# A state-space mixer inside a two-layer decoder: SiLU through Tanh, decay tiles prepared group by group, and a new order of the projections around z

## The chip, the cores and the metric

The kernel runs on one core of one Trainium2 chip. The metric is the device time of one execution in microseconds (us); lower is better. A core has five engines that run side by side, each through its own queue in order: TensorE (PE in the profile, with its weight loads shown apart as PEld), VectorE (DVE), ScalarE (ACT), GpSimd (POOL), and SyncE (SP), whose queue issues most transfers. An instruction waits at the head of its queue until what it needs is there, and everything behind it waits too.

## The reference

A trunk of two layers works on 256 tokens of 1024 features, all in 32-bit floats. Each layer is FFN, token mixer, cross-attention into 256 memory tokens, FFN. The mixer of layer 0 is differential attention. That of layer 1 is a Mamba-2 state-space mixer, and the change lies there alone:

```python
proj = h @ w_in                                   # 1024 -> 2048 z, 2048 xs, 1024 B, 1024 C, 32 dt
xbc = silu(causal_depthwise_conv(xbc, conv_w, conv_b))       # 4 taps along time
dt = softplus(dt + dt_bias); A = -exp(A_log)
a_cs = cumsum(dt * A) within chunks of 128 tokens
decay = exp(where(tril, a_cs[l] - a_cs[s], -inf))            # 32 heads x 2 chunks x 128 x 128
y_diag = (C B^T * decay) @ (xs * dt)                         # 8 groups of 4 heads share B and C
states = B^T (exp(a_cs[-1] - a_cs) * dt * xs);  y_off = exp(a_cs) * (C @ states of the chunk before)
y = (y_diag + y_off + D * xs) * silu(z)
y = y * rsqrt(mean over each group's 256 features of y^2 + eps) * gnorm;  return y @ w_out
```

## The kernel before

All products of weights run at full precision as three matmuls: a weight piece `w` is split into a rounded `whi` (ScalarE, L183) and the difference `wlo = w - whi` (VectorE, L184), and likewise the activations. Such a piece is 128x1024 elements and is called a gran here. Four `whi` and four `wlo` buffers and four weight buffers `w` rotate; a weight buffer is free for the next load when its pieces have been split, and SyncE's queue issues the loads in order. `proj` and `wide` (L199 on) append units, each a list of grans and a function with the matmuls; `proj` takes an `eng`, on which the difference of a unit's second gran is then made.

In the mixer (`ssd`), layer 1 runs 4 rounds. Round i serves groups 2i and 2i+1. It projects b and c for both groups (256 columns each), then xs (two units of 256 columns, one a group), then z for both. The small work on each group hangs on a planner, `pipe`: `pipe.after(us, f)` puts f into the program that many microseconds of planned matmul time later. The order of TensorE's instructions is exactly the order in which they are written, through these delays. The order on the other engines is set by the scheduler of the tile library at build time.

The steps of a group g, with the names that the profile shows:

- `conv`: ScalarE scales the newest tap out of PSUM (L1035), VectorE adds three older taps for each of two halves (L1042, 128x255, 254, 253), ScalarE applies SiLU with the bias (L1047). This is done for b, c (per round) and xs (per group).
- The decay tiles `E`, 128x512 for each group and chunk, come from a small DRAM buffer `scr` through SyncE's queue (L1006). ScalarE turns them with four `Relu` (L1020, 128x128 each) and one `Exp` (L1024).
- `cross` on TensorE: `tb` turns b, `pcb` is C B^T (L1096, L1101). VectorE masks it to `cbm` (L1107) and multiplies it into both E tiles (L1109).
- `turn_x`: TensorE turns xs into `tx` (L1116), ScalarE copies it to `xn` (L1120), GpSimd makes `xd = xn*dt`, `xe = xd*dte` and `xn*D` (L1124 to L1128).
- `inner`: `pst` (the state) and `py` (L1137, L1142). `state`: `pof` (L1156). `gate`: the sums and the product with `zs` = SiLU(z) (L1090, L1163 to L1165), the squares, `yrc` (a power on GpSimd, L315), the scaling, and `turn_y` with `ty` (L1185), whose result `y_hi`, `y_lo` feeds the output projection `out`.

SiLU, Exp and Tanh are evaluated from function tables in ScalarE; where the next function is not in the loaded set, the build puts an ACT_TABLE_LOAD before it.

Of the kernel before, what the change touches and what calls it, by code (L numbers as in the profile page):

```python
# [15 lines left out]
P = 128  # L16
# [41 lines left out]
def trunk(ctx, tc, a, out):  # L58
# [251 lines left out]
    def rpow(src, scale, n, name):  # L310

        m = sm.tile([P, 16], F32, name="msq", tag="msq")
        nc.vector.tensor_scalar(m[:, :n], src, scale, EPS, op0=ALU.mult, op1=ALU.add)  # L313
        c = sm.tile([P, 16], F32, name=name, tag=name)
        nc.gpsimd.tensor_tensor(c[:, :n], m[:, :n], neghalf[:, :n], op=ALU.pow)  # L315
        return c
# [593 lines left out]
    def ssd(norm, nxt, kv):  # L910
# [8 lines left out]
        dte = const.tile([P, 32], F32, name="dte")  # L919
        E = {}  # L920
# [29 lines left out]
        def dt_steps(pd):  # L950
            xd = const.tile(d32, F32, name="dtx")
            u = const.tile(d32, F32, name="dtu")
            s = const.tile(d32, F32, name="dts")
            s2 = const.tile(d32, F32, name="dts2")
            nega = const.tile([P, 32], F32, name="nega")
            for t in range(2):
                v.tensor_tensor(xd[:, t, :], pd[t], dtb, op=ALU.add)

            v.scalar_tensor_tensor(u, xd, -1.0, xd, op0=ALU.mult, op1=ALU.min)
            tc.keep_in_program_order(nc.scalar.activation(nega, alog, AF.Exp))  # L960

            def second():
                nc.scalar.activation(u, u, AF.Exp)
                pipe.after(1.0, third)

            def third():
                v.tensor_scalar(s, u, 2.0, None, op0=ALU.add)
                v.reciprocal(s, s)
                v.tensor_tensor(s, s, u, op=ALU.mult)
                v.tensor_tensor(s2, s, s, op=ALU.mult)  # L970
                v.tensor_scalar(dt, s2, 2.0 / 17, None, op0=ALU.mult)
                for c in (15, 13, 11, 9, 7, 5, 3):
                    v.scalar_tensor_tensor(dt, dt, 2.0 / c, s2, op0=ALU.add, op1=ALU.mult)
                v.scalar_tensor_tensor(dt, dt, 2.0, s, op0=ALU.add, op1=ALU.mult)
                v.scalar_tensor_tensor(dt, xd, 0.0, dt, op0=ALU.max, op1=ALU.add)
                v.scalar_tensor_tensor(av, dt, -1.0, nega.unsqueeze(1).broadcast_to(d32), op0=ALU.mult, op1=ALU.mult)
                pipe.after(5.0, sums)
            pipe.after(1.0, second)

        def sums():  # L980
# [9 lines left out]
            def out_of_psum():  # L990
# [35 lines left out]
        def conv(ps, ch, name, wait):  # L1026
# [18 lines left out]
            def silu():  # L1045
                for j in range(2):
                    nc.scalar.activation(o[:, j, :], o[:, j, :], AF.Silu, bias=cb_[:, ch[j]:ch[j] + 1])  # L1047
            pipe.after(evac, taps)
            pipe.after(wait, silu)
            return o  # L1050

# [22 lines left out]
        def group(g):  # L1074
# [3 lines left out]
            def xs_fin(ps):  # L1078
                s["xs"] = conv(ps, (2 * g, 2 * g + 1), "xs", 6.5)
                if g == 0:  # L1080
                    s["zs"] = held.pop()
                    pipe.after(6.5, lambda: nc.scalar.activation(s["zs"], s["zs"], AF.Silu))
                pipe.after(9.5, turn_x)

            def z_fin(ps):
                zs = v2(slot("zs"))

                def go():
                    for t in range(2):
                        nc.scalar.activation(zs[:, t, :], ps[t], AF.Silu)  # L1090
# [3 lines left out]
            def cross():  # L1094
# [8 lines left out]
                def go():  # L1103
                    s["bn"] = work("bn", P)
                    nc.scalar.copy(s["bn"], tb[:, 0:P])
                    cbm = work("cbm", S).rearrange("p (c l) -> p c l", c=2)
                    v.tensor_tensor(cbm, pcb[:, 0:2, :], triu.unsqueeze(1).broadcast_to([P, 2, P]), op=ALU.mult)  # L1107
# [4 lines left out]
            def turn_x():  # L1112
# [5 lines left out]
                def go():  # L1118
# [10 lines left out]
                                            dsk[:, hs].unsqueeze(1).unsqueeze(3).broadcast_to(bh), op=ALU.mult)  # L1129
                    s.update(xn=xn, xd=xd, xe=xe)  # L1130
                    pipe.after(8.5, inner)
                pipe.after(evac, go)

            def inner():
# [10 lines left out]
                def go():  # L1145
# [4 lines left out]
                    pipe.when(2.5, lambda: "zs" in s, state)  # L1150
                pipe.after(evac, go)

            def state():
# [7 lines left out]
                def gate():  # L1161
                    yo = work("yo", S)
                    v.tensor_tensor(r4(yo), r4(pof), b4(eacs[:, hs]), op=ALU.mult)  # L1163
# [13 lines left out]
                pipe.after(evac + 7.0, lambda: rc.append(rpow(ss[:, 0:2], 1.0 / 256, 2, "yrc")))  # L1177
# [188 lines left out]
```

## Time and profile before

| | |
|---|---|
| median of 3 runs | 1316.27 us (1316.23 to 1316.58) |
| the profiled execution | 1315.35 us, its span in the profile 1313.6 us |
| TensorE busy | 1296.7 us of the span (99%) |
| VectorE, ScalarE, GpSimd busy | 807.7, 738.5, 67.8 us (61%, 56%, 5%) |
| granted TensorE clock, mean | 0.996 |
| the mixer of layer 1 | about 798 us to 1035 us of the span |

A busy share near 1 on TensorE over the whole span says that a change elsewhere can matter only where TensorE stands still or runs at a lower clock. The queries used are: busy time by stretches of the span, the waits of TensorE, the groups of instructions by line, and the timeline of single engines. In a row of a group, the numbers behind the bar are total busy time and the mean of one instruction in ns, and behind the second bar the idle time of the engine just before them with what ended it.

### The profile page before, as it was taken

Reading aid. Unit: us, or ns where it says so; the run is one execution under the profiler, and the core shown is the slowest. Engines: PE = TensorE matmul, PEld = TensorE weight load, DVE = VectorE, ACT = ScalarE, POOL = GpSimd, SP = SyncE. Lnnn points to the kernel's source line nnn. Section 1 sums busy time; section 2 is a strip of 40 time slices with the busy share of each in tenths; the row PEclk is TensorE's granted clock in tenths of the full one; section 3 lists DMA queues with packets and bytes.
Section 4 is the critical chain, followed back from the end, with each engine's and each line's share of the span. In section 5 each row is a group of like instructions: output and inputs, shape, how many; then the busy total and the mean of one; then the engine's idle time right before and its main releaser. Section 6 shows DMA issues by size and latency. Waiting matters only on the chain.

```text
span 1313.6 us, 17832 instructions
## 1 busy us (share of the span) xinstructions
PE 1296.7 (99%) x6997; PEld 1115.4 (85%) x6997; DVE 807.7 (61%) x1178; ACT 738.5 (56%) x1208; POOL 67.8 (5%) x67
## 2 busy tenths in 40 slices
PE   9999999999999999999999999989999999999998
PEld 7888888788988888888888889889998898888887
DVE  5655456876665555555556456667885775655554
ACT  6456444685455444445445447999774664544432
POOL 1000002210000000000000000022311000000000
PEclk9999999999999999999999999999999999999999
DMA  9565565425445554656555546744534445655551
GB/s 325 187 219 182 178 198 173 154 102 191 161 142 176 186 173 130 234 182 217 172 186 189 187 152 216 225 156 129 186 136 160 161 161 161 197 173 175 208 177 49
DMA packets 134631, 232.02 MB, mean 177 GB/s; under 512 B 5737, under 2 KB 34066, under 8 KB 134546
## 3 DMA queue, kind: packets, MB, share of 16 engines
q1 hardware_dynamic: 133648, 229.75, 53.2%
q8 instruction: 55, 0.90, 0.3%
q10 hardware_dynamic: 738, 0.59, 0.1%
q0 software_dynamic: 160, 0.52, 0.1%
q14 instruction: 30, 0.25, 0.0%
HBM read 229.77 MB, written 1.08 MB: 176 GB/s over the span
## 4 chain that ended last, share of the span: by engine, by line
PE 88%; ACT 6%; DVE 3%; issue 1%; POOL 1%; DMA 1%; SPq 0%; POOLq 0%; ACTq 0%; DVEq 0%
PE out L221 7%; PE out L223 7%; PE out L222 7%; PE up L222 6%; PE up L223 6%; PE up L221 6%; PE gate L223 5%; PE gate L221 5%; PE gate L222 5%; ACT whi L183 2%; PE htp L611 1%; PE fin L221 1%; PE fin L223 1%; PE fin L222 1%; PE xq L222 1%
## 5 line engine op out<-in xcount | busy, mean ns | idle before, releaser
L184 DVE TENSOR_TENSOR wlo<-w,whi 128x1024 fp32r<-128x1024 f32 (+2 forms) x446 | 523.7, 1180 | 415.4 <-ACT whi L183 413.7
L183 ACT CAST whi<-w 128x1024 fp32r<-128x1024 f32 (+1 forms) x448 | 447.6, 1006 | 473.3 <-PE out L223 147.0
L222 PE MATMUL up<-wlo,xh 128*128 128x512 f32 x320 | 124.7, 390 | 0.1
L223 PE MATMUL up<-whi,xl 128*128 128x512 f32 x320 | 124.6, 389 | 0.0
L221 PE MATMUL up<-whi,xh 128*128 128x512 f32 x320 | 124.6, 389 | 0.0
L221 PE MATMUL gate<-whi,xh 128*128 128x512 f32 x312 | 123.3, 395 | 0.0
L222 PE MATMUL gate<-wlo,xh 128*128 128x512 f32 x312 | 121.7, 390 | 0.0
L223 PE MATMUL gate<-whi,xl 128*128 128x512 f32 x312 | 121.7, 390 | 0.0
L221 PE MATMUL out<-whi,hid_hi 128*128 128x512 f32 x264 | 103.6, 392 | 0.0
L223 PE MATMUL out<-whi,hid_lo 128*128 128x512 f32 x264 | 102.9, 390 | 0.0
L222 PE MATMUL out<-wlo,hid_hi 128*128 128x512 f32 x264 | 102.9, 390 | 0.0
L222 PEld LDWEIGHTS up<-wlo,xh 128*128 128x128 f32 x320 | 60.1, 188 | 13.0 <-DVE wlo L184 0.5
L221 PEld LDWEIGHTS up<-whi,xh 128*128 128x128 f32 x320 | 60.1, 188 | 12.5
L223 PEld LDWEIGHTS up<-whi,xl 128*128 128x128 f32 x320 | 60.1, 188 | 12.4
L223 PEld LDWEIGHTS gate<-whi,xl 128*128 128x128 f32 x312 | 58.6, 188 | 12.2
L222 PEld LDWEIGHTS gate<-wlo,xh 128*128 128x128 f32 x312 | 58.7, 188 | 11.9 <-POOL wlo L184 0.4
L221 PEld LDWEIGHTS gate<-whi,xh 128*128 128x128 f32 x312 | 58.7, 188 | 11.5
L223 PEld LDWEIGHTS out<-whi,hid_lo 128*128 128x128 f32 x264 | 49.6, 188 | 10.4
L222 PEld LDWEIGHTS out<-wlo,hid_hi 128*128 128x128 f32 x264 | 49.6, 188 | 10.0
L221 PEld LDWEIGHTS out<-whi,hid_hi 128*128 128x128 f32 x264 | 49.6, 188 | 10.0
L315 POOL TENSOR_TENSOR rcol<-msq,neghalf 128x2 f32<-128x2 f32 x8 | 5.6, 696 | 686.8 <-DVE msq L313 686.8
L221 PE MATMUL fin<-whi,hid_hi 128*128 128x512 f32 (+1 forms) x110 | 38.3, 348 | 0.0
(354 smaller groups left out, 2735.9 us busy)
## 6 DMA issues: line engine op xcount, KB each, us to landing
w<-in_ffn_w_up_dram SPq DMA_DIRECT2D x40, 1024.0 KB, 5.0
w<-in_ffn_w_down_dram SPq DMA_DIRECT2D x40, 1024.0 KB, 5.0
w<-in_ffn_w_gate_dram SPq DMA_DIRECT2D x38, 1024.0 KB, 5.0
w<-in_ssd_w_in_dram SPq DMA_DIRECT2D x24, 1024.0 KB, 5.3
w<-in_xa_w_kv_dram SPq DMA_DIRECT2D x16, 1024.0 KB, 5.0
w<-in_da_w_in_dram SPq DMA_DIRECT2D x12, 1024.0 KB, 5.1
w<-in_xa_w_q_dram SPq DMA_DIRECT2D x8, 1024.0 KB, 5.1
w<-in_xa_w_o_dram SPq DMA_DIRECT2D x8, 1024.0 KB, 4.9
```

The lines of the kernel that those rows point to most:

```text
L183: nc.scalar.copy(hv, src)
L184: self.eng.tensor_tensor(self.lo[:, :, o:o + n], src, hv.bitcast(F32), op=ALU.subtract)
L221: nc.tensor.matmul(o, lhsT=lh, rhs=rh, start=start, stop=False)
L222: nc.tensor.matmul(o, lhsT=lh, rhs=rl, start=False, stop=False)
L223: nc.tensor.matmul(o, lhsT=ll, rhs=rh, start=False, stop=stop)
L315: nc.gpsimd.tensor_tensor(c[:, :n], m[:, :n], neghalf[:, :n], op=ALU.pow)
L611: nc.tensor.transpose(tp[:, j, t * P:(t + 1) * P], us[t][:, (i + j) * P:(i + j + 1) * P], ident)
```

## The change

1. SiLU(x) is computed as x/2 times (1 + tanh(x/2)). The factor one half is left out of the products and put elsewhere: dt, D and the copies of b and of C B^T carry it (`dt*0.5`, `dskh`, `bn*0.5`, `0.25` at cbm, `0.5` at yo, and the normalization's eps times 4). One ScalarE Tanh of 128x512 and one VectorE product of 128x512 (`th`, L1064 and L1065 of the changed kernel) stand for two SiLU of 128x256. For z there are two Tanh and two products of 128x256 (L1059, L1061). The conv's bias moves into the first tap.
2. The decay tiles of group g are loaded 16 planned us before a time `at` of their own and turned just before it; before, groups 0 to 3 went first, all together.
3. The second group's xs stands behind z in rounds 0 to 2, and xs weights come in two loads of 256 columns.
4. The difference of the second gran of each b and c unit is made on GpSimd (8 grans).
5. The delays: b's SiLU after 6.5 in place of 12.3, `cross` after 12.0 and 18.0 more (6.0 in the last round) in place of 10.0 and 2.5, `turn_x` after 11.5 in place of 9.5, `state` after 3.2 in place of 2.5.

```diff
-                    pipe.after(0.5 if g < 4 else 24.0 + 7.0 * (g - 4), lambda g=g: spread(g))
+                    at = (9.0, 36.0, 47.0, 64.5, 80.5, 98.0, 114.0, 120.0)[g]
+                    pipe.after(max(0.5, at - 16.0), lambda g=g: spread(g))
                     for c in range(2):
-                        i = 2 * g + c
-                        pipe.after(6.0 + 1.3 * i if g < 4 else 33.0 + 4.0 * (i - 8), lambda g=g, c=c: decay(g, c))
-                    pipe.after((14.0, 16.0, 33.5, 36.0, 67.5, 70.0, 72.5, 75.0)[g], lambda g=g: decay2(g))
+                        pipe.after(max(6.0, at - 4.5) + 1.5 * c, lambda g=g, c=c: decay(g, c))
+                    pipe.after(at, lambda g=g: decay2(g))
...
-                    nc.scalar.activation(o[:, j, :], ps[:, j, :], AF.Copy, scale=tap(3, j))
+                    nc.scalar.activation(o[:, j, :], ps[:, j, :], AF.Identity, scale=tap(3, j),
+                                         bias=cb_[:, ch[j]:ch[j] + 1])
...
-            def silu():
-                for j in range(2):
-                    nc.scalar.activation(o[:, j, :], o[:, j, :], AF.Silu, bias=cb_[:, ch[j]:ch[j] + 1])
             pipe.after(evac, taps)
-            pipe.after(wait, silu)
+            pipe.after(wait, lambda: silu2(o, o, o, v))
             return o
+
+        def silu2(dst, src, keep, eng):
+            th = work("th")
+            if isinstance(src, list):
+                for t in range(2):
+                    nc.scalar.activation(th[:, t * S:(t + 1) * S], src[t], AF.Tanh, scale=0.5)
+                for t in range(2):
+                    v.scalar_tensor_tensor(dst[:, t, :], th[:, t * S:(t + 1) * S], 1.0, src[t], op0=ALU.add, op1=ALU.mult)
+            else:
+                th = v2(th)
+                nc.scalar.activation(th, src, AF.Tanh, scale=0.5)
+                eng.scalar_tensor_tensor(dst, th, 1.0, keep, op0=ALU.add, op1=ALU.mult)
...
-                t = conv(ps, (ch, ch + 1), which, 12.3 if which == "b" else 6.7)
+                t = conv(ps, (ch, ch + 1), which, 6.5)
...
-                        pipe.after(10.0 + 2.5 * j, crosses[g])
+                        pipe.after(12.0 + (6.0 if i == 3 else 18.0) * j, crosses[g])
...
-                    pipe.after(6.5, lambda: nc.scalar.activation(s["zs"], s["zs"], AF.Silu))
-                pipe.after(9.5, turn_x)
+                    pipe.after(1.0, lambda: silu2(s["zs"], s["zs"], s["zs"], v))
+                pipe.after(11.5, turn_x)
...
-                    pipe.after(8.5, inner)
+                    pipe.when(8.5, lambda: "bn" in s, inner)
...
-                    pipe.when(2.5, lambda: "zs" in s, state)
+                    pipe.when(3.2, lambda: "zs" in s, state)
...
-            proj("a", w_in, 4096 + 256 * i, 256, norm, "b", [bc_fin(i, "b")])
-            proj("a", w_in, 5120 + 256 * i, 256, norm, "c", [bc_fin(i, "c")])
-            proj("a", w_in, 2048 + 512 * i, 512, norm, "xs", fx)
+            proj("a", w_in, 4096 + 256 * i, 256, norm, "b", [bc_fin(i, "b")], eng=nc.gpsimd)
+            proj("a", w_in, 5120 + 256 * i, 256, norm, "c", [bc_fin(i, "c")], eng=nc.gpsimd)
+            def xs(j):
+                proj("a", w_in, 2048 + 512 * i + 256 * j, 256, norm, "xs", [fx[j]])
+            xs(0)
+            if i == 3:
+                xs(1)
...
+            if i < 3:
+                xs(1)
```

How the instructions stand. First ScalarE's queue before, from behind the copy of the first turn of xs to the SiLU of xs that the second turn waits for:

```order
L1024 ACT_TABLE_LOAD
L1024 ACTIVATE E<-E 128x512
L1090 ACT_TABLE_LOAD
L1090 ACTIVATE zs<-z 128x256
L1047 ACTIVATE xs<-xs,cols_111 128x256
L1090 ACTIVATE zs<-z 128x256
L183 CAST whi<-w 128x1024
L1024 ACT_TABLE_LOAD
L1024 ACTIVATE E<-E 128x512
L183 CAST whi<-w 128x1024
L1047 ACT_TABLE_LOAD
L1047 ACTIVATE xs<-xs,cols_111 128x256
```

The same queue in the changed kernel, from the first group's Tanh (`th` from xs) to the second's; the Relu of L1024 right behind `xn` is the first of group 2:

```order
L1064 ACTIVATE th<-xs 128x512
L1059 ACTIVATE th<-z 128x256 x2
L183 CAST whi<-w 128x1024 x2
L1134 COPY xn<-tx 128x512
L1024 ACTIVATE E<-E,acs 128x128
L1039 ACTIVATE xs<-xs,cols_111,cols_112 128x256 x2
L1024 ACTIVATE E<-E,acs 128x128 x2
L183 CAST whi<-w 128x1024
L1024 ACTIVATE E<-E,acs 128x128 x5
L1028 ACTIVATE E<-E 128x512
L1039 ACTIVATE b<-b,cols_111,cols_112 128x256 x2
L1064 ACTIVATE th<-xs 128x512
```

The table loads are gone (7 in the whole program in place of 23), and one Relu of group 2 now stands ahead of the taps of the second xs.

Then SyncE's queue of the changed kernel, where the decay tiles (E from scr) stand among the loads of weights (w). In brackets is what a row waits for; w_7771 takes the buffer of w_7406, whose second half GpSimd reads:

```order
L161 DMA w_7406<-in_ssd_w_in_dram 128x8x256 [waits DMAHW6_49,Pool_49]
L161 DMA w_7490<-in_ssd_w_in_dram 128x8x256 [waits DMAHW7_49,DVE_49]
L161 DMA w_7577<-in_ssd_w_in_dram 128x8x256 [waits DMAHW0_49,DVE_49]
L1010 DMA E_7358<-scr_7100 128x4x128 [waits PE_49]
L1010 DMA E_7360<-scr_7100 128x4x128 [waits DMAHW1_49,PE_49]
L161 DMA w_7666<-in_ssd_w_in_dram 128x4x512 [waits DVE_49]
L161 DMA w_7771<-in_ssd_w_in_dram 128x4x512 [waits DMAHW3_49,DMAHW5_49,DVE_49,Pool_49]
L1010 DMA E_7512<-scr_7100 128x4x128 [waits DMAHW4_49,PE_49]
```

Group 2's tiles (E_7512) now follow a weight load that waits for GpSimd; before, the first four groups' tiles went out in one block behind `scr`.

Last, GpSimd's queue of the changed kernel in round 2 (groups 2 and 3 still being finished):

```order
L184 TENSOR_TENSOR wlo<-w,whi 128x1024
L1138 TENSOR_TENSOR xd<-xn,dt 128x512
L1141 TENSOR_TENSOR xe<-xd,dte 128x256
L1142 TENSOR_TENSOR xn<-xn,dskh 128x512
L315 TENSOR_TENSOR yrc<-msq,neghalf 128x2
L184 TENSOR_TENSOR wlo<-w,whi 128x1024
```

Before, the same place holds only `xd`, `xe`, `xn` and `yrc`; the two weight differences of b and c stand around them now.

More of the change, by code (lines that the diff above doesn't have):

```diff
@@ L308, in split_act, with rpow @@
             nc.vector.scalar_tensor_tensor(l_, s_, c_, h_.bitcast(F32), op0=ALU.mult, op1=ALU.subtract)
-    def rpow(src, scale, n, name):
+    def rpow(src, scale, n, name, eps=EPS):
         m = sm.tile([P, 16], F32, name="msq", tag="msq")
-        nc.vector.tensor_scalar(m[:, :n], src, scale, EPS, op0=ALU.mult, op1=ALU.add)
+        nc.vector.tensor_scalar(m[:, :n], src, scale, eps, op0=ALU.mult, op1=ALU.add)
         c = sm.tile([P, 16], F32, name=name, tag=name)
@@ L919, in ssd @@
         dte = const.tile([P, 32], F32, name="dte")
+        dskh = const.tile([P, 32], F32, name="dskh")
         E = {}
@@ L1088, in go @@
                 def go():
-                    for t in range(2):
-                        nc.scalar.activation(zs[:, t, :], ps[t], AF.Silu)
+                    silu2(zs, ps, None, v)
                     s["zs"] = zs
@@ L1104, in go @@
                     s["bn"] = work("bn", P)
-                    nc.scalar.copy(s["bn"], tb[:, 0:P])
+                    nc.scalar.mul(s["bn"], tb[:, 0:P], 0.5)
                     cbm = work("cbm", S).rearrange("p (c l) -> p c l", c=2)
-                    v.tensor_tensor(cbm, pcb[:, 0:2, :], triu.unsqueeze(1).broadcast_to([P, 2, P]), op=ALU.mult)
+                    v.scalar_tensor_tensor(cbm, pcb[:, 0:2, :], 0.25, triu.unsqueeze(1).broadcast_to([P, 2, P]),
+                                           op0=ALU.mult, op1=ALU.mult)
                     for c in range(2):
@@ L1162, in gate @@
                     yo = work("yo", S)
[L1163 removed]
+                    v.scalar_tensor_tensor(r4(yo), r4(pof), 0.5, b4(eacs[:, hs]), op0=ALU.mult, op1=ALU.mult)
                     v.tensor_tensor(y[:, 1, :], y[:, 1, :], yo, op=ALU.add)
@@ L1176, in state @@
                 pipe.after(evac + 4.5, square)
-                pipe.after(evac + 7.0, lambda: rc.append(rpow(ss[:, 0:2], 1.0 / 256, 2, "yrc")))
+                pipe.after(evac + 7.0, lambda: rc.append(rpow(ss[:, 0:2], 1.0 / 256, 2, "yrc", 4 * EPS)))
                 pipe.after(evac + 10.0, scale)
```

4 lines of the change are left out of this document (3 added, 1 removed).

## The prediction

> **What bounds the kernel now.** I read the page first, then busy time by stretches, TensorE's waits, and ScalarE's timeline where they fall.
>
> ```profile
> span 1313.6 us, 17832 instructions
> PE 1296.7 (99%) x6997; PEld 1115.4 (85%) x6997; DVE 807.7 (61%) x1178; ACT 738.5 (56%) x1208; POOL 67.8 (5%) x67
> ```
>
> TensorE is the bound, and no matmul is added or removed. Only its standing still can be won. The mixer by stretches (busy time of PE, PEld, DVE, ACT, POOL, then the granted clock, DMA share, GB/s):
>
> ```profile
> 812.00:835.00 23.00, 22.77 (x189) 22.36 (x189) 13.79 (x27) 17.67 (x44) 0.00 (x0) 1.00 0.72 220
> 835.00:880.00 45.00, 37.56 (x282) 36.33 (x281) 29.94 (x49) 42.74 (x80) 7.22 (x6) 0.92 0.62 194
> 880.00:925.00 45.00, 45.00 (x329) 42.48 (x329) 34.63 (x61) 41.59 (x83) 9.15 (x8) 1.00 0.42 133
> 925.00:970.00 45.00, 44.76 (x328) 42.03 (x327) 37.10 (x61) 30.32 (x63) 10.87 (x9) 1.00 0.49 165
> 970.00:1000.00 30.00, 30.00 (x169) 25.91 (x168) 21.82 (x33) 17.95 (x33) 6.97 (x7) 1.00 0.44 148
> ```
>
> TensorE misses 0.23, 7.44, 0, 0.24 and 0 us, 7.9 in all, nearly all of it in 835 to 880, where ScalarE is busy 42.74 of 45. Its waits there:
>
> ```profile
> PE tx L1116 <- ACT xs L1047: 5.4, 3, 4.8
> PE tb L1096 <- ACT b L1047: 1.1, 1, 1.1
> PE xs L223 <- DVE wlo L184: 0.7, 1, 0.7
> PE pcb L1101 <- ACT c L1047: 0.5, 1, 0.5
> ```
>
> 7.0 of 7.7 us wait for a SiLU. The longest, 4.8, is seen on ScalarE:
>
> ```profile
> 852.71 1.28 ACT L1024 ACT_TABLE_LOAD   x1
> ...
> 859.25 0.63 ACT L1024 ACTIVATE E<-E 128x512 f32<-128x512 f32 x1
> 860.83 1.28 ACT L1047 ACT_TABLE_LOAD   x1
> 862.13 0.51 ACT L1047 ACTIVATE xs<-xs,cols 128x256 f32<-128x256 f32 x1
> ```
>
> The first and the last of four loads, 5.1 us of the ten before the SiLU that ends the wait. Standing still costs a second time, in the clock:
>
> ```profile
> 838.70:842.10 3.40, 1.72 (x11) 1.39 (x11) 1.76 (x2) 3.37 (x6) 0.00 (x0) 1.00 0.50 129
> 842.20:845.50 3.30, 2.87 (x13) 2.87 (x14) 1.73 (x3) 3.30 (x7) 0.00 (x0) 0.50 0.99 338
> 862.70:866.00 3.30, 3.30 (x16) 3.30 (x17) 0.00 (x0) 3.29 (x6) 0.87 (x1) 0.50 0.83 277
> 866.10:869.50 3.40, 3.40 (x31) 3.40 (x30) 2.21 (x4) 3.40 (x11) 1.68 (x3) 1.00 0.00 0
> ```
>
> After each bout of waiting the clock is half for 3.4 us: 16 matmuls where 31 go at full clock, 15 x 0.11 = 1.65 us lost, and some 13 x 0.11 = 1.4 in the other. So 7.7 + 3.1 = 10.8 us are at stake.
>
> A rule of the Trainium skill bears on the 3.1: "TensorE: Matmul & The Clock Gate", Part 1, has the clock fall only after a whole idle window of about 3.4 us. By it the wait of 1.1 would have cost no clock, 9.4 us would be at stake, and new short waits would cost only themselves. The trace differs: the stretch ahead of the first fall had TensorE at work for 1.72 of 3.40 us, and I keep 10.8.
>
> **The change, part by part.** What each piece costs (the second row is ScalarE's time in the Relu line L1020 alone in that stretch):
>
> ```profile
> 818.92 3.75 DMA E<-scr
> 822.60:862.60 40.00, 11.52 (x36) 0.96 0.69 215
> L1024 ACT ACT_TABLE_LOAD x6 | 7.7, 1283 | 0.1
> L1047 ACT ACT_TABLE_LOAD x5 | 6.4, 1283 | 0.1
> L1047 ACT ACTIVATE xs<-xs,cols 128x256 f32<-128x256 f32 x16 | 8.1, 504 | 2.4 <-DVE xs L1042 2.4
> 828.35 2.46 ACT L1020 ACTIVATE E<-E,acs 128x128 f32<-128x128 f32 x8
> L183 ACT CAST whi<-w 128x1024 fp32r<-128x1024 f32 x52 | 54.2, 1047 | 22.6 <-PE z L223 4.9 <-PE b L222 4.6 <-PE out L223 4.5
> L1174 ACT ACTIVATE y<-y,yrc 128x256 f32<-128x256 f32 x12 | 5.7, 504 | 2.4 <-POOL yrc L315 2.4
> L184 DVE TENSOR_TENSOR wlo<-w,whi 128x1024 fp32r<-128x1024 f32 x402 | 495.9, 1236 | 396.9 <-ACT whi L183 395.3
> L976 DVE SCALAR_TENSOR_TENSOR av<-dt,nega 128x64 f32<-128x64 f32 x1 | 0.2, 224 | 0.0
> L184 POOL TENSOR_TENSOR wlo<-w,whi 128x512 fp32r<-128x512 f32 x2 | 2.6, 1296 | 8.5 <-ACT whi L183 8.5
> L1128 POOL TENSOR_TENSOR xn<-xn,vec 128x512 f32<-128x512 f32 x8 | 10.6, 1325 | 0.1
> E<-scr SPq DMA_DIRECT2D x16, 256.0 KB, 5.3
> ```
>
> *Tables.* 16 loads go, 16 x 1.28 = 20.5 us of ScalarE. Where ScalarE hides behind TensorE this is worth nothing. Between the first E tile's landing (818.92 + 3.75 = 822.7) and the second turn (862.6) it is on the path: five loads, 6.4 us.
>
> *Decay by group.* ScalarE did 36 Relu and six Exp in that stretch. Ahead of the second turn's xs there now stand 24 and five: 12 x 0.31 (eight in 2.46) = 3.7 and 0.6 us less. With the loads 10.7 us leave ScalarE's queue ahead of waits of 7.0. The Relu come back later, where ScalarE has lost its other eleven loads.
>
> *SiLU.* Two of 504 ns become one Tanh of 128x512, nearest the Exp of that shape, 0.63: 0.4 less on ScalarE. VectorE gets 17 products of 128x512 and 14 of 128x256 and loses eight differences. The products appear in no row: at the least as an addition that reads PSUM or a lone E product, 0.64, at the most like one that collides with GpSimd, 1.26 (rows below). I take 0.69 and 0.48, as the wider and the narrower products around them: 11.7 + 6.7 - 8 x 1.24 = +8.5 us on VectorE, hidden while it is below TensorE. The halves in dt and D are two products of at most 64 columns, 0.22 each, in a stretch (812 to 835) where VectorE is busy 13.8 of 23.
>
> *xs weights* come in two loads of the same bytes each; with DMA shares of 0.42 to 0.72 that is hidden.
>
> *GpSimd's eight pieces.* 128x1024 appears nowhere on GpSimd. Twice the row of 128x512 is 2.6 us, twice the fastest xd (1.04) 2.1, twice the slowest copy (2.02) 4.0. I take 2.6 to 3.5 and keep both ends.
>
> ```profile
> 848.84 1.28 DVE L1109 TENSOR_TENSOR E<-E,cbm 128x512 f32<-128x512 f32 x2
> 937.76 1.04 POOL L1124 TENSOR_TENSOR xd<-xn,dt 128x512 f32<-128x512 f32 x1 [8.72 <-ACT xn L1120]
> 937.85 2.52 DVE L1109 TENSOR_TENSOR E<-E,cbm 128x512 f32<-128x512 f32 x2
> 939.79 1.48 POOL L1128 TENSOR_TENSOR xn<-xn,vec 128x512 f32<-128x512 f32 x1
> 940.29 0.47 DVE L1042 SCALAR_TENSOR_TENSOR xs<-xs,cols 128x254 f32<-128x254 f32 x1
> 940.69 1.66 DVE L184 TENSOR_TENSOR wlo<-w,whi 128x1024 fp32r<-128x1024 f32 x1
> 947.35 2.02 POOL L1128 TENSOR_TENSOR xn<-xn,vec 128x512 f32<-128x512 f32 x1
> ```
>
> *Is each wait gone, and what is late next?* I follow the queues by hand on a clock whose 0 is the first matmul of the unit with dt (798.6) and on which TensorE never waits (0.12 us a narrow matmul). One instruction takes about 0.1 less than its row where the next follows at once.
> (a) `pcb` of group 0 moves from 40.0 to 42.15. ScalarE starts on E at 24, does eight Relu (2.4), two taps, two Exp (1.1) and three casts, and reaches c's taps at 31. VectorE's six taps with two differences between them end at 37.3; Tanh and product make c ready at 39.5: 2.6 us to spare.
> (b) `tx` of group 0 (now 47.4): VectorE has `cbm` at 43.1, two E products to 44.75, the product for xs to 45.4: 2.0 to spare.
> (c) Group 2's E. The b piece reaches GpSimd at 42.6 and is done by 45.2 (46.6 at 4.0). Only then does the weight load ahead of E go out, and E lands 5.3 later, at 51.7. ScalarE has been at that Relu since 49.0: 2.7 us idle, with the second xs's taps, and so VectorE, behind it. The second `tx` (60.4) still has its xs at 58.2, but both engines stay 3 us behind: in round 1 the xs of group 2 is ready at 80.8 to 80.9 against a `tx` at 80.1. A new wait of 0.8.
> (d) c's piece in rounds 2 and 3 stands on GpSimd behind b's piece, xd, xe, xn and yrc, and its cast on ScalarE behind scalings that need yrc: two of 0.4, two roundings alike and the cast of 0.95 are 2.5. A set of xd, xe, xn and yrc takes 4.0 to 4.6 (seven in 6.97 us, eight in 9.15). From b's cast (82.6 in round 2): 2 x 2.6 + 4.0 + 2.5 = 11.7, so 94.3 against a use at 97.0, after the shift of 0.8. At 3.5 a piece and 4.6 it is 96.7, just in time.
>
> *The sum*, on the profiled execution's 1315.35 us: less 10.8, plus 0.8 for (c) and 0.4 for smaller waits, is 1305.75. The median lies 0.92 above that execution, so 1306.7 us.
>
> **Rivals.**
> *GpSimd is the slow link.* At 4.0 us a piece, (d) becomes 8 + 6 (xd and xn at 2.0, xe at half of it, yrc 1) + 2.5 = 16.5 from 82.6, 99.1, so 2.1 late, in two rounds; E in (c) lands 1.4 later and its wait grows to 2.2. That is 4.2 + 1.4, and half clock after each (1.5 x 3): 10.1 at the worst, 1316.8; half of it, 1311.7, is the likelier. For it: GpSimd's copies took 1.04 alone and 2.02 beside VectorE. Against it: its queue is idle four fifths of the mixer. It decides from about 3.5 us a piece.
> *VectorE becomes the bound* (slower). E products go from 0.64 to 1.26 and a difference takes 1.66 in place of 1.24 when GpSimd runs beside them; a tap, which reads PSUM, keeps 0.47. VectorE is busy 123.5 us of 835 to 1000; with 8.5 more it has 132 of the 154 that remain. If all 33 wide products (0.62 each) and some 44 differences (0.42) collided, 39 us would come on top, 17 over: 1306.7 + 17 = 1324. It sets the time from 22 us of collisions, and makes the kernel slower than before from about 32. Against it: GpSimd works 34 us of the mixer now and some 58 then, a third of the time, so about 13.
> The Trainium skill ("GPSIMD Engine Reference", Specifications) says that GpSimd shares its SBUF interfaces with VectorE and contends with instructions that read two SBUF inputs. The new products of conv's results are of that kind, the taps are not; the rows above agree.
> *The waits only change their name.* If xs, now two engines' work after the taps, is as late as its SiLU was, TensorE loses the same 7 to 11 us: 1315 to 1317. Against it: 10.7 us leave ScalarE's queue there, and (a) and (b) have 2 us to spare.
>
> **How the numbers follow.** The forecast (1304 to 1309) has 0.62; GpSimd as the slow link (1309 to 1313.6) 0.22; the waits renamed 0.09; VectorE as the bound, with the worst of GpSimd, 0.07. All waits gone and nothing new is 1305.5, and some small matmul gaps below the listed waits could go too, so the low end is 1304. The high end is 1313: beyond it lie the last two cases and the tail of the second. Within 0.2% (2.6 us, about what a measurement of this kernel can tell from no change) means 1313.6 to 1318.9. Faster 0.84, same 0.09, slower 0.07.
>
> **What would show it.** TensorE's busy time in 835 to 880 above 44 of 45, and no half clock there; no table load between 800 and 1060; ScalarE's waits for E's transfer near 2.7 us in round 0; GpSimd's pieces at 2.6 to 3.5 us; VectorE 5 to 10 points busier from 880 on. The prediction is wrong if `tx`, `pcb` or a matmul on `wlo` from GpSimd waits several us in each round, or if VectorE stands above 95% there.

## The result, and the profile after

The changed kernel takes 1305.07 us (median of 4 runs, 1305.00 to 1305.66) against 1316.25 (4 runs, 1316.03 to 1316.58), 11.2 us less. The ratio on record is 0.9921, with a 95% interval of 0.9908 to 0.9933; the two medians alone divide to 0.9915. The profiled execution took 1305.0 us, so here it stands at the median. Its page:

```profile
span 1302.8 us, 17812 instructions
PE 1292.9 (99%) x6997; PEld 1111.4 (85%) x6997; DVE 822.3 (63%) x1203; ACT 715.4 (55%) x1176; POOL 89.9 (7%) x75
```

The mixer by stretches, in the columns of the prediction (PE, PEld, DVE, ACT, POOL, granted clock, DMA share, GB/s):

```profile
812.00:835.00 23.00, 21.55 (x179) 21.13 (x178) 15.16 (x28) 14.47 (x27) 4.83 (x2) 1.00 0.63 197
835.00:880.00 45.00, 45.00 (x349) 43.52 (x348) 38.90 (x65) 33.17 (x69) 12.27 (x9) 1.00 0.65 199
880.00:925.00 45.00, 45.00 (x321) 42.05 (x320) 39.58 (x65) 35.64 (x79) 14.09 (x10) 1.00 0.54 165
925.00:970.00 45.00, 45.00 (x343) 43.18 (x342) 39.97 (x71) 34.81 (x76) 15.34 (x10) 1.00 0.56 183
970.00:1000.00 30.00, 30.00 (x158) 25.46 (x158) 23.73 (x34) 16.50 (x33) 10.34 (x8) 1.00 0.44 148
```

From 835 on TensorE does not stand still and its clock does not fall. It misses 1.45 us in these stretches, where it missed 7.9 before; with the two half clock stretches that are gone (some 3.1 us) this is 9.6 of the 10.8 us by which the span is shorter. The rows of the two pages split the whole 10.8: TensorE is busy 3.8 us less (1296.7 to 1292.9), as matmuls at half clock take longer, and stands still 7.0 us less. In the list of waits all entries for `tx`, `tb` and `pcb` are gone. One is new (total, times, longest), and one of ScalarE answers to point (c) of the prediction:

```profile
PE acs L987 <- issue: 1.5, 1, 1.5
ACT E L1024 <- DMA E<-scr: 3.6, 3, 3.1
```

Among the groups of ScalarE's instructions between 800 and 1000 there is one table load left:

```profile
L961 ACT ACT_TABLE_LOAD x1 | 1.3, 1283 | 0.0
```

`acs`, which is newly waited for, is the running sum of the decay's exponents. GpSimd's timeline shows what comes ahead of it (start, duration):

```profile
812.14 2.41 POOL L184 TENSOR_TENSOR wlo<-w,whi 128x1024 fp32r<-128x1024 f32 x1 [22.89 <-DVE dt L974]
```

And the timelines of VectorE and, in the last row, of TensorE:

```profile
812.18 2.46 DVE L974 SCALAR_TENSOR_TENSOR dt<-dt,dts 128x64 f32<-128x64 f32 x1
...
816.49 0.23 DVE L977 SCALAR_TENSOR_TENSOR av<-dt,nega 128x64 f32<-128x64 f32 x1
816.82 0.41 PE L987 MATMUL acs<-av,cst 128*128 128x64 f32 x2 [1.45 <-issue]
```

GpSimd's first weight difference starts at 812.14 and ends at 814.55. One step of the polynomial for dt, 0.23 us elsewhere, starts 0.04 us behind it and ends at 814.64: VectorE stood until GpSimd was done. `av` is then ready 1.4 us later than before (815.11 there), and TensorE waits for it. The Trainium skill ("SBUF — State Buffer", SBUF: two separate sides) has it so: a GpSimd instruction that reads SBUF and a VectorE instruction with two SBUF inputs exclude each other, and the later one blocks for the whole of the earlier. The 2.46 beside 2.41 agrees.

### The profile page after: what moved, and what is told of

Same layout as the page of the kernel before. It is cut to its first block, busy times and chain, and to the rows that moved or that the text cites. A ratio compares the mean times of both kernels' runs of the same rounds, so it can differ in the third digit from the quotient of the medians.

```text
span 1302.8 us, 17812 instructions
## 1 busy us (share of the span) xinstructions
PE 1292.9 (99%) x6997; PEld 1111.4 (85%) x6997; DVE 822.3 (63%) x1203; ACT 715.4 (55%) x1176; POOL 89.9 (7%) x75
## 4 chain that ended last, share of the span: by engine, by line
PE 96%; DVE 2%; ACT 1%; DMA 1%; issue 0%; POOL 0%; POOLq 0%; ACTq 0%
PE out L223 7%; PE out L221 7%; PE out L222 7%; PE up L222 6%; PE up L223 6%; PE up L221 6%; PE gate L223 5%; PE gate L221 5%; PE gate L222 5%; PE xs L221 1%; PE htp L611 1%; PE xs L223 1%; PE xs L222 1%; PE fin L222 1%; PE fin L223 1%; PE fin L221 1%
## 5 line engine op out<-in xcount | busy, mean ns | idle before, releaser
L184 DVE TENSOR_TENSOR wlo<-w,whi 128x1024 fp32r<-128x1024 f32 (+2 forms) x438 | 513.8, 1178 | 401.6 <-ACT whi L183 399.8
L221 PEld LDWEIGHTS up<-whi,xh 128*128 128x128 f32 x320 | 60.1, 188 | 12.5
L222 PEld LDWEIGHTS gate<-wlo,xh 128*128 128x128 f32 x312 | 58.7, 188 | 12.5 <-DVE wlo L184 0.5
L223 PEld LDWEIGHTS gate<-whi,xl 128*128 128x128 f32 x312 | 58.5, 188 | 12.3
L221 PEld LDWEIGHTS gate<-whi,xh 128*128 128x128 f32 x312 | 58.6, 188 | 11.5
L223 PEld LDWEIGHTS out<-whi,hid_lo 128*128 128x128 f32 x264 | 49.5, 188 | 10.3
L221 PEld LDWEIGHTS out<-whi,hid_hi 128*128 128x128 f32 x264 | 49.5, 188 | 10.1
```

Source lines behind the costliest of these rows:

```text
L184: self.eng.tensor_tensor(self.lo[:, :, o:o + n], src, hv.bitcast(F32), op=ALU.subtract)
L221: nc.tensor.matmul(o, lhsT=lh, rhs=rh, start=start, stop=False)
L222: nc.tensor.matmul(o, lhsT=lh, rhs=rl, start=False, stop=False)
L223: nc.tensor.matmul(o, lhsT=ll, rhs=rh, start=False, stop=stop)
```

## The experiments

The main parts of the change were each taken out of the changed kernel, and some were put alone into the kernel before. The two loads of the xs weights, the later C B^T and the bias in the first tap were not taken out by themselves. The theories: T, the table loads in ScalarE's queue are the loss; D, the order of the decay's work is; O, the room ahead of the turns (delays, second xs behind z) is what takes the waits away; G and C, on whether GpSimd's share helps or costs. A summary first; the median of before was 1315.0 to 1315.7 beside these runs.

| kernel | us | ratio to before, 95% |
|---|---|---|
| before + Tanh and product | 1322.26 | 1.0058 (1.0045 to 1.0071) |
| before + Tanh, no product | 1313.01 | 0.9985 (0.9977 to 0.9994) |
| before + decay's order | 1307.09 | 0.9947 (0.9930 to 0.9963) |
| before + decay's order, C B^T late enough | 1309.50 | 0.9962 (0.9949 to 0.9976) |
| changed | 1305.07 | 0.9921 (0.9908 to 0.9933) |
| changed, Silu kept | 1312.57 | 0.9981 (0.9972 to 0.9989) |
| changed, no product | 1304.56 | 0.9923 (0.9911 to 0.9935) |
| changed, old decay order | 1314.39 | 0.9993 (0.9985 to 1.0002) |
| changed, xs before z | 1312.95 | 0.9975 (0.9966 to 0.9985) |
| changed, three old delays | 1313.61 | 0.9985 (0.9977 to 0.9994) |
| changed, first GpSimd piece on VectorE | 1304.47 | 0.9919 (0.9907 to 0.9931) |
| changed, no GpSimd pieces | 1303.16 | 0.9905 (0.9890 to 0.9919) |
| changed, GpSimd pieces twice | 1316.86 | 1.0010 (1.0001 to 1.0018) |

### SiLU by Tanh alone, and the loads alone

The kernel before with Tanh and product in place of Silu (and the bias and the halves moved as in the change):

```diff
-                    nc.scalar.activation(o[:, j, :], o[:, j, :], AF.Silu, bias=cb_[:, ch[j]:ch[j] + 1])
...
+                nc.scalar.activation(th, src, AF.Tanh, scale=0.5)
+                eng.scalar_tensor_tensor(dst, th, 1.0, keep, op0=ALU.add, op1=ALU.mult)
```

> Only the SiLU by Tanh is taken from the change (with the bias moved into the first tap and the halves in the scales); the decay's order, the delays, the order of xs and z and the subtractions stay as before. Theory T (the table loads in ScalarE's queue ahead of the second turn are the main loss): 16 of 23 loads go, 5 of 1.28 us each of them (6.4 us) between 822.7 and 862.6, so 1316.3 - 6.4 = 1309.9, between 1309 and 1311. Theory D (the order of the decay's work is the main loss): the decays of groups 0 to 3 still stand ahead of the second turn, so at most 1 to 2 us go: 1314.5 to 1315.5. Theory O (the later turn, cross and second xs are what removes the wait): the turn still comes at its old place and waits, 1314 to 1316.

It took 1322.26 us, 0.58% more than before: no theory had it. Its stretches:

```profile
835.00:880.00 45.00, 38.92 (x315) 37.61 (x313) 37.91 (x62) 42.24 (x95) 6.33 (x6) 1.00 0.68 212
880.00:925.00 45.00, 42.15 (x292) 39.06 (x291) 36.50 (x64) 27.85 (x53) 9.45 (x9) 0.96 0.38 121
925.00:970.00 45.00, 42.71 (x298) 39.75 (x297) 36.84 (x62) 26.48 (x50) 7.85 (x8) 0.96 0.41 132
```

TensorE's longest entry in its list of waits:

```profile
PE tx L1130 <- DVE xs L1065: 10.7, 5, 2.8
```

The end of one of these waits in the timelines of ScalarE, VectorE and TensorE:

```profile
850.93 0.63 ACT L1064 ACTIVATE th<-xs 128x512 f32<-128x512 f32 x1
851.60 0.69 DVE L1065 SCALAR_TENSOR_TENSOR xs<-th,xs 128x512 f32<-128x512 f32 x1 [0.39 <-ACT th L1064]
852.35 0.66 PE L1130 MATMUL tx<-ident,xs 128*128 128x128 f32 x4 [1.24 <-DVE xs L1065]
```

No load stands in ScalarE's queue in the rounds here, yet TensorE waits at five turns, in every round, for the product. The turn comes 9.5 us behind the projection, and the way taps, Tanh, product does not fit in. Clock is lost behind two of the waits. To part the loads from the link, the next kernel has Tanh in the very instructions of Silu and no product, so it leaves SiLU itself out (one of three places is shown):

```diff
-                        nc.scalar.activation(zs[:, t, :], ps[t], AF.Silu)
+                        nc.scalar.activation(zs[:, t, :], ps[t], AF.Tanh)
```

> The kernel before with Tanh in place of Silu in the mixer, in the same instructions, and no product: SiLU itself is left out, so the table loads go (7 for 23) and nothing is added on VectorE. It prices the loads by themselves, where the run with Tanh and the product was 6 us slower than before. Theory T: the five loads between 822.7 and 862.6 are worth 6.4 us, 1315.7 - 6.4 = 1309.3, between 1308 and 1311, and the added link of Tanh and product then costs 1322.3 - 1309.3 = 13 us in the old order. Theory Q (in the old order the decay in ScalarE's queue decides, loads or not): 1313.5 to 1316, and the link costs 6 to 9 us.

1313.01 us: 2.4 less than before. Neither theory's range held it, and it lies nearer to Q. The stretch of the second turn, and then the longest wait of TensorE:

```profile
835.00:880.00 45.00, 41.14 (x335) 40.02 (x334) 34.75 (x58) 43.65 (x100) 8.24 (x7) 1.00 0.65 208
```

```profile
PE tx L1116 <- ACT xs L1047: 5.3, 3, 2.5
```

With the loads out ScalarE is still busy 43.65 of 45 us there, and the turns wait 5.3 us in all, as before (5.4). But they are not the same waits. The second turn's falls from 4.76 to 2.48 us and leaves no half clock behind it; a new one, of 2.40, stands in round 1, with a clock of 0.96 in 880 to 925. The timelines of ScalarE and TensorE show where it comes from:

```profile
894.00 0.91 ACT L1174 ACTIVATE y<-y,yrc 128x256 f32<-128x256 f32 x2 [2.77 <-POOL yrc L315]
896.31 0.55 PE L1116 MATMUL tx<-ident,xs 128*128 128x128 f32 x3 [2.40 <-ACT xs L1047]
```

The build put the SiLU of this xs (895.75) behind a scaling that waits 2.77 us for GpSimd's `yrc`; in the kernel before such a SiLU stands ahead of it. So in the old order taking the loads out gains 2.4 us net. The new wait and its lost clock come to an estimated 2.4 + 45 x 0.04 = 4.2 us, so without them the loads would be near T's 6.4; no run shows that. The link of Tanh and product costs 1322.26 - 1313.01 = 9.3 (by the ratios 0.73%, 9.6).

### The decay's order alone

```diff
-                    pipe.after(0.5 if g < 4 else 24.0 + 7.0 * (g - 4), lambda g=g: spread(g))
+                    at = (9.0, 36.0, 47.0, 64.5, 80.5, 98.0, 114.0, 120.0)[g]
+                    pipe.after(max(0.5, at - 16.0), lambda g=g: spread(g))
...
```

> The kernel before with the changed order of the decay's work alone (spread, decay and decay2 by group); Silu and its table loads, delays, projections and subtractions as before. T: the decay's 4.3 us leave ScalarE's queue ahead of the second turn, the loads stay, so 1316.3 - 4.3 = 1312.0, between 1311 and 1314 (the 4.3 us count only if they really stood between the turn and what it needs). D: most of the 10.8 us go, 1306 to 1309. O: no more than 1 us goes, 1315 to 1316.5.

1307.09 us. In it the products with C B^T come ahead of the decay, so a wait that the real kernel has is missing, and the time is a lower bound. The next one has the later C B^T that the order needs:

```diff
-                        pipe.after(10.0 + 2.5 * j, crosses[g])
+                        pipe.after(12.0 + (6.0 if i == 3 else 18.0) * j, crosses[g])
...
-                    pipe.after(8.5, inner)
+                    pipe.when(8.5, lambda: "bn" in s, inner)
```

> The kernel before with the changed order of the decay's work and, since that needs it, the changed delay of C B^T (inner waits for bn as changed); Silu, projections, turns and subtractions as before. It mends the run with the decay's order alone, in which the products with C B^T came ahead of the decay they multiply, and which took 1307.1. Theory D (the decay ahead of the second turn is the main loss in the order before): 1306 to 1309. Theory T (the loads count as much as the prediction said, and 29 of them stand here for 23 before): 4.3 us go and some come back, 1311 to 1315.

1309.50 us, 5.9 less than before: just above D's range and well below T's, and more than the 4.3 us that the prediction gave the decay, though 29 table loads stand here for 23. What waits in it, in a profiled execution of 1311.83 us:

```profile
PE tx L1116 <- ACT xs L1047: 2.5, 2, 2.2
PE py L1142 <- DVE E L1109: 1.2, 1, 1.2
```

### Silu kept, in the changed order

Silu is back on ScalarE, without product and halves; one of two places is shown:

```diff
-                nc.scalar.activation(th, src, AF.Tanh, scale=0.5)
-                eng.scalar_tensor_tensor(dst, th, 1.0, keep, op0=ALU.add, op1=ALU.mult)
+                nc.scalar.activation(dst, src, AF.Silu)
```

> The changed kernel with ScalarE's own Silu put back (the bias stays in the first tap, the halves are taken out), so that 31 table loads stand where 7 did; all orders, delays and GpSimd's subtractions stay as changed. T: the loads come back into ScalarE's queue; 5 loads (6.4 us) between 822.7 and 862.6 would return, 1305.1 + 6.4 = 1311.5, between 1309 and 1313, and VectorE gets some 8 us shorter without gain. D and O: the orders carry the change, and it stays within 1.5 us of the changed kernel: 1304 to 1306.6.

1312.57 us (11 runs, 1309.78 to 1314.97), as T expected, but at other places than T has them. The profiled execution is the fastest of the eleven, 1309.78. Its groups of table loads, then one of its stretches, then TensorE's three waits:

```profile
L1059 ACT ACT_TABLE_LOAD x12 | 15.4, 1283 | 0.2
L1027 ACT ACT_TABLE_LOAD x10 | 12.8, 1283 | 0.2
```

```profile
925.00:970.00 45.00, 44.31 (x337) 41.86 (x335) 32.82 (x55) 44.63 (x87) 13.28 (x10) 1.00 0.55 172
```

```profile
PE out L222 <- DVE wlo L184: 2.2, 1, 2.2
PE acs L986 <- issue: 1.3, 1, 1.3
PE pof L1164 <- ACT state L1155: 1.2, 1, 1.2
```

In 835 to 880 TensorE misses nothing. The decay, spread over all rounds, alternates with Silu in each, so 22 loads fill ScalarE's queue to 44.63 of 45 us in 925 to 970. The wait of 1.2 is for a copy (970.25) that stands behind a load (968.42). The wait of 2.2 is not ScalarE's: the cast for it ends at 984.3, and the difference stands on VectorE until 985.3 behind two products, which take 2.98 us together (1.28 alone) while GpSimd is at work:

```profile
982.36 2.98 DVE L1117 TENSOR_TENSOR E<-E,cbm 128x512 f32<-128x512 f32 x2
```

The loads are worth 7.5 us in the new order and 2.4 in the old one. The trace accounts for 4.8 of the 7.5 (1309.78 against 1305.0); the rest is in executions that were not profiled, nine of which have a mean clock of 0.995 to 0.997 where this one has 0.999.

### The product left out, in the changed order

This kernel leaves SiLU out, and Tanh is written in its place; one of the two products is shown:

```diff
-                v.scalar_tensor_tensor(dst[:, t, :], th[:, t * S:(t + 1) * S], 1.0, src[t], op0=ALU.add, op1=ALU.mult)
```

> The changed kernel without VectorE's products of SiLU (Tanh is written where SiLU stood; SiLU itself is left out); loads, orders, delays and GpSimd's pieces as changed. It prices the added link in the new order. If the new order hides it: within 0.8 us of the changed kernel, 1304.3 to 1305.6, since the one wait left (acs, 1.5 us) comes ahead of any SiLU. If VectorE's added 8.5 us still show: 1301 to 1304.

1304.56 us against 1305.07. The engines' row of its page, and then its only wait in the mixer:

```profile
PE 1292.8 (99%) x6997; PEld 1112.9 (85%) x6997; DVE 806.3 (62%) x1172; ACT 715.3 (55%) x1176; POOL 91.1 (7%) x75
```

```profile
PE acs L987 <- issue: 1.4, 1, 1.4
```

VectorE is 16.0 us shorter and the time 0.5: the link that cost 9.3 us in the old order is hidden in the new one.

### The order and the room, each taken out

The old order of the decay in the changed kernel (the lines of the diff above, reversed):

> The changed kernel with the decay's work in its old order (groups 0 to 3 ahead of the second turn); Tanh, delays, xs behind z and GpSimd's pieces as changed. Theory D (4.3 us of decay ahead of the second turn come back as a wait there, with half clock behind it): 1308 to 1313. Theory O (the later turn and z's matmuls cover them): 1304.8 to 1306.

1314.39 us: above D's range, and no longer to be told from before (0.9985 to 1.0002). The profiled execution took 1315.09; the stretch of the first two turns, that of the last round, and then the two longest waits:

```profile
835.00:880.00 45.00, 40.78 (x313) 39.56 (x311) 39.00 (x57) 41.24 (x88) 11.40 (x8) 0.96 0.66 201
970.00:1000.00 30.00, 28.20 (x138) 23.32 (x137) 26.59 (x41) 17.41 (x34) 8.84 (x7) 0.94 0.44 149
```

```profile
PE tx L1130 <- DVE xs L1065: 2.9, 1, 2.9
PE pcb L1114 <- DVE c L1065: 1.8, 1, 1.8
```

The first turn waits 2.9 us, since the decay of four groups stands ahead of the taps of xs on ScalarE, which start at 843.6 here and at 837.8 in the changed kernel. D had the wait at the second turn, which has none. TensorE misses 4.2 and 1.8 us in the two stretches and loses an estimated 45 x 0.04 + 30 x 0.06 = 3.6 by the clock: 9.6 of the 10.3 us by which the span is longer than the changed kernel's. Next, both pieces of xs ahead of z in all rounds:

```diff
             xs(0)
-            if i == 3:
-                xs(1)
+            xs(1)
```

> The changed kernel with both projections of xs ahead of z in all rounds, as before, in two pieces; all else as changed. Theory O (the second turn of a round has no wait because z's matmuls stand between it and its projection): the second xs is then turned while ScalarE and VectorE still work on the first, and TensorE waits 1 to 3 us in each of rounds 0 to 2, so 1308 to 1313. Theory T with D (loads and decay out of the way are enough): 1304.5 to 1306.

1312.95 us: O has the size, but not the place. Of its waits, beside the one for `acs`, only the third is a turn:

```profile
PE py L1156 <- DVE E L1123: 1.7, 2, 1.3
PE pst L1151 <- ACT bn L1118: 0.6, 1, 0.6
PE tx L1130 <- DVE xs L1065: 0.5, 1, 0.5
```

Without z in between, the second group's inner products come before its C B^T has been through the engines: in round 2 `pcb` is done at 947.8, but ScalarE's copy `bn` comes at 951.6, behind decay work for which it had waited 5.1 us on the transfer of E (until 944.1). The mean clock in 925 to 970 is 0.92 in this kernel: so behind waits of 2 us there an estimated 45 x 0.08 = 3.6 us of clock are lost. Last, three delays as before:

```diff
-                t = conv(ps, (ch, ch + 1), which, 6.5)
+                t = conv(ps, (ch, ch + 1), which, 12.3 if which == "b" else 6.7)
...
-                pipe.after(11.5, turn_x)
+                pipe.after(9.5, turn_x)
...
-                    pipe.when(3.2, lambda: "zs" in s, state)
+                    pipe.when(2.5, lambda: "zs" in s, state)
```

> The changed kernel with three delays as before: SiLU of b 12.3 us behind its projection (6.5 as changed), the turn of xs 9.5 us behind (11.5), the state 2.5 us (3.2). The delay of C B^T stays as changed, since the decay's new order needs it. From the run with Tanh alone, where TensorE waited 10.7 us in five turns for VectorE's product of xs: theory O (the added link, Tanh and then a product, is what the later turn makes room for) has each turn 2 us early and so up to 1 us of wait in each of eight turns, 1308 to 1313; theory D (the old order of the decay alone made the turns wait, and with the new one the link fits in 9.5 us) has 1304.5 to 1306.5. The b delay alone could put a wait of 1 to 3 us at the turn of b.

1313.61 us, just above O's range. The two longest entries beside `acs`:

```profile
PE tx L1130 <- DVE xs L1065: 4.1, 5, 1.5
PE pcb L1114 <- DVE c L1065: 0.9, 1, 0.9
```

Five turns wait for the product, as with Tanh alone. The turn of b does not. Whether the 0.7 us of the state matters was not tried apart.

### GpSimd's pieces

The first piece moved back to VectorE, all of them moved back, or each done twice:

```diff
-            proj("a", w_in, 4096 + 256 * i, 256, norm, "b", [bc_fin(i, "b")], eng=nc.gpsimd)
+            proj("a", w_in, 4096 + 256 * i, 256, norm, "b", [bc_fin(i, "b")], eng=nc.gpsimd if i else None)
```

> The changed kernel with one difference: the second half of b's weight difference of round 0 is subtracted on VectorE, not on GpSimd (seven pieces stay there). In the changed kernel this piece runs on GpSimd from 812.14 to 814.55 beside the softplus chain of dt on VectorE (545 ns each for seven, 224 ns before), and TensorE then waits 1.45 us for acs in front of L987, which it did not before. Theory C (GpSimd's piece slows the chain that acs waits for): the wait goes back to 0.2, 1305.1 - 1.3 = 1303.8, between 1303.3 and 1304.2. Rival (the chain is later because of work in another order on VectorE, not for GpSimd's piece): the wait stays, 1304.8 to 1305.4, or grows, as VectorE gets 1.3 us more just there.

1304.47 us (1303.50 to 1305.17). The group of the polynomial's steps (545 ns each in the changed kernel), and then the waits of TensorE:

```profile
L974 DVE SCALAR_TENSOR_TENSOR dt<-dt,dts 128x64 f32<-128x64 f32 x7 | 1.6, 224 | 0.2
```

```profile
PE acs L987 <- issue: 0.2, 1, 0.2
PE pcb L1114 <- DVE c L1065: 0.8, 1, 0.8
```

C is right about `acs`: with the piece gone, so is the wait. The time is just above C's range: a new wait of 0.8 us at 921 gives part of it back, and the runs overlap those of the changed kernel (1305.00 to 1305.66). There c was ready at 921.51 and `pcb` came at 921.57, so the wait for `acs` had covered this one. With no pieces on GpSimd at all (the line of b changes likewise):

```diff
...
-            proj("a", w_in, 5120 + 256 * i, 256, norm, "c", [bc_fin(i, "c")], eng=nc.gpsimd)
+            proj("a", w_in, 5120 + 256 * i, 256, norm, "c", [bc_fin(i, "c")])
```

> The changed kernel with all weight differences on VectorE again (the eight pieces of 128x1024 leave GpSimd: 19.4 us less there, 8 x 1.26 = 10.1 us more on VectorE); everything else as changed. Theory G (GpSimd's share is needed, since with SiLU's products VectorE would be the bound): more than half of the added time shows, 1308 to 1315. Theory C (its pieces are worth nothing, and the first one costs the 1.3 us wait for acs): 1305.1 - 1.3 = 1303.8, between 1303.3 and 1304.8. Neither: 1304.8 to 1306.

1303.16 us (4 runs, 1302.99 to 1303.31), just below C's range and the fastest of all, 1.9 below the changed kernel (by the ratios 0.16%, 2.1). The engines' row of its page, and then the one wait in the mixer:

```profile
PE 1292.7 (99%) x6997; PEld 1112.3 (85%) x6997; DVE 825.3 (63%) x1211; ACT 716.0 (55%) x1176; POOL 72.9 (6%) x67
```

```profile
PE acs L987 <- issue: 0.2, 1, 0.2
```

G falls: VectorE gets eight differences back, 8 x 1.26 = 10.1 us, but its busy time grows by 3.0 only. The other 7.1 us, net, were time for which its instructions stood behind GpSimd's: with the pieces gone, the steps for dt take 2.2 us less in all, the sums with `yo` 2.2, the products with `zs` 1.7 and those with E 1.9. All of these read two SBUF inputs; the sum with `py`, which reads PSUM, keeps its 683 ns. Twice the work on GpSimd:

```diff
...
-                self.eng.tensor_tensor(self.lo[:, :, o:o + n], src, hv.bitcast(F32), op=ALU.subtract)
+                for _ in range(2 if self.twice and self.nk * n == 1024 else 1):
+                    self.eng.tensor_tensor(self.lo[:, :, o:o + n], src, hv.bitcast(F32), op=ALU.subtract)
```

> The changed kernel with each of GpSimd's eight subtractions done twice in place, so that a piece takes 4.85 instead of 2.42 us (and VectorE's work beside it is slowed for twice as long). The prediction had GpSimd decide from about 3.5 us a piece, with 10 us late at 4.0. If that holds: 1312 to 1320. Rival (the queue of weight pieces runs far enough ahead to hide it; only the first piece shows, by the chain for acs): 1305.1 plus 0.5 to 2.5, 1305.6 to 1307.6.

1316.86 us at 4.9 us a piece: inside the expected range, and at what the prediction's rival had as the worst for 4.0. GpSimd's pieces and the polynomial's steps by groups, and then the two longest waits:

```profile
L186 POOL TENSOR_TENSOR wlo<-w,whi 128x1024 fp32r<-128x1024 f32 x16 | 39.3, 2455 | 68.2 <-ACT whi L184 44.8 <-DVE dt L976 22.9
L976 DVE SCALAR_TENSOR_TENSOR dt<-dt,dts 128x64 f32<-128x64 f32 x7 | 6.0, 856 | 0.2
```

```profile
PE pcb L1116 <- DVE c L1067: 4.1, 1, 4.1
PE acs L989 <- issue: 3.6, 1, 3.6
```

But TensorE waits for VectorE's results, `av` and c, and not for GpSimd's differences. Ahead of the wait of 4.1, in round 3, the trace shows two delays: ScalarE stands 3.2 us for a `yrc` that follows a double piece on GpSimd, a link that point (d) of the prediction has, and a difference on VectorE takes 3.25 us beside the next double piece. So GpSimd's time is paid in a late `yrc` and a blocked VectorE, not in late weights; how much each costs was not tried apart.

## Why the prediction was right, and where it was not

The time was 1305.07 where 1306.7 was forecast: 0.75 us lie in the sum (1305.75 for the profiled execution, 1305.0 measured), the other 0.85 in the distance from there to the median, 0.92 before and 0.07 after.

*10.8 us at stake.* Nearly: with no GpSimd pieces, in the kernel that waits least, the span is 12.5 us shorter than before (1301.1 to 1313.6), so 1.7 us more could go than the sum held: 8.5 us of standing still for 7.7, and 4.0 of busy time for the 3.1 of half clock. Some 0.4 of it lies in the first 50 us, outside the mixer.

*Tables, 6.4 us, and decay, 4.3.* The waits that the two were to end did end, but the terms are not the prices. Put in alone, the loads are worth 2.4 us net of a new wait and the decay's order 5.9; left out of the changed kernel alone, 7.5 and 9.3. No run has the two without the rest. The failing step is the assumption that what leaves ScalarE's queue leaves the wait too, term by term. A turn waits for the later of several chains, and behind each of these changes stands another one that is nearly as late.

*SiLU's product, hidden.* Right only together with the later turn (0.5 us there, 9.3 in the old order). Points (a) and (b) counted with the later turn but gave it no price of its own; the old delays alone bring 8.5 us back. Durations were near: 683 to 752 ns for the wide product (0.69 taken) and 410 for the narrow (0.48).

*(a), (b) and (d).* No turn, C B^T or weight of GpSimd is waited for. In (a) 3.1 us were to spare (2.6 forecast), but in (b) only 0.3 of the 2.0: the two E products took 3.21 us in place of 1.65, beside a GpSimd piece (844.34 to 846.75), and xs was ready at 848.50 for a turn at 848.79. On the hand clock of the prediction this piece (42.6 to 45.2) and the products (43.1 to 44.75) overlap too, but it put the collision at nothing there. That this turn did not wait is partly luck; with the pieces twice as long it waits 1.4. *(c)* ScalarE waits 3.1 us for the transfer of E (2.7 forecast), but the wait of 0.8 at round 1's turn that should follow does not come. By the clock of the prediction the turn was due at 878.7 and its xs at 879.5; they came at 885.0 and 883.35. So TensorE was 6.3 us behind the hand clock (1.45 of it the wait for `acs`) and xs only 3.9.

*GpSimd's pieces.* 2.42 us each, below the 2.6 to 3.5 taken and inside the bounds. That they are harmless below 3.5 us was wrong: at 2.42 they cost 1.9 us. The step that failed is the placing: the first piece falls on the chain for dt, which the prediction looked at only for its two added products. This wait of 1.45 happens to replace the 0.8 + 0.4 of the sum.

*VectorE as the bound.* It did not come: 39.97 of 45 us at the most. From 880 to 1000 it is busy 103.3 of 120 us, 93.6 before, 8 points more, as forecast. The 13 us estimated were for collisions with all of GpSimd's work. The eight pieces alone brought some 7; no run shows the whole.

*What would show it.* Full busy time and no half clock in 835 to 880: seen. A table load between 800 and 1060: one stands at L961, in the work on dt ahead of the mixer's rounds, off TensorE's path.

## What to carry to other kernels

When an engine waits for a chain that crosses several queues, removing one cause shows little until the next one is gone as well: here parts that take 2 to 6 us off, or add 7, when put in alone are each worth 7 to 9 us in the whole. So undo each part of a bundle in the full kernel, and do not add up their separate gains. Work given to GpSimd is not free for VectorE: check which short VectorE chain runs at that moment, and who waits for its end.

## What the runs showed of the hardware

A GpSimd instruction can stop a VectorE instruction altogether (0.23 us became 2.46). A short TensorE wait does not always cost clock. The changed kernel and the one with old delays have the same wait of 1.45 us ahead of `acs` at the same time, and these are the stretches with it and behind it, first of the changed kernel:

```profile
815.10:818.50 3.40, 1.95 (x16) 1.53 (x15) 3.16 (x12) 0.23 (x1) 0.00 (x0) 1.00 0.79 238
818.50:821.90 3.40, 3.40 (x31) 3.40 (x30) 0.14 (x2) 1.76 (x3) 1.20 (x1) 1.00 0.34 109
```

And of the one with old delays:

```profile
815.10:818.50 3.40, 1.95 (x16) 1.58 (x15) 3.19 (x11) 0.23 (x1) 0.00 (x0) 1.00 0.82 261
818.50:821.90 3.40, 3.40 (x19) 3.40 (x18) 0.03 (x1) 1.76 (x3) 0.73 (x1) 0.50 0.33 100
```

31 matmuls against 19 in the same 3.4 us. The Trainium skill ("TensorE: Matmul & The Clock Gate", Part 1) says that the window in which activity is counted runs freely, so that its phase differs from run to run; these two rows fit that, but its whole idle window does not, with TensorE at work 1.95 of the 3.40 us ahead of the fall. It also fits that kernels that wait scatter (1308.74 to 1314.45 with xs before z) where the one with hardly a wait (no GpSimd pieces) stays within 0.4 us. That the phase is the cause was not tried.
